# Feature-major projections as seven block products, in three passes of tokens

## The chip, the cores and the metric

The kernel runs on one core of one Trainium2 chip. TensorE (PE) multiplies: a matmul takes 128 rows of a stationary operand (loaded by LDWEIGHTS, the rows PEld of the profile) and streams up to 512 columns past it into a bank of PSUM, 128 x 512 numbers of fp32. VectorE (DVE), ScalarE (ACT) and GpSimd (POOL) work element by element, SyncE (SP) only issues DMAs. SBUF is the working memory; POOL does not touch PSUM in this kernel. Every engine has its own queue and runs it in order; semaphores join them.

The metric is device time in microseconds of one execution.

## What is computed

One layer on 2048 prompt tokens and 32 sample tokens, fp32:

```python
h = jnp.einsum('bsd,de->bse', x, w_in)              # 1024 -> 6 x 512
u, v, ga, bv, bg, gb = jnp.split(h, ...)
u = gelu(u); v = layer_norm(gelu(v), a_ln_g, a_ln_b)
y_a = u * spatial_gating(v, a_ws, a_bias) * silu(ga) # 128-token chunks, 8 heads
a = bv * sigmoid(bg)
c, new_hist = depthwise_causal_conv(conv_hist, a, b_conv_w, b_conv_b)   # 31 taps
y_b = silu(layer_norm(c, b_ln_g, b_ln_b)) * silu(gb)
y = jnp.einsum('bse,ed->bsd', concatenate([y_a, y_b]), w_out)
x_new = layer_norm(ALPHA * x + y, post_ln_g, post_ln_b)
```

Outputs are the new tokens, the last 30 convolution rows of both groups and the normalised v rows of the sample.

## The kernel before

Every fp32 operand of a product is split into a high part (an ACT copy to fp32r) and a low part (the rest, a subtraction on DVE or POOL), and a product is three matmuls: high with high, high with low, low with high.

The tokens lie in four groups of 512, 544, 512 and 512 (the sample in the second). Two halves of two groups each are worked through one after the other. In each half come the v products of the first group (token-major, `mm_v`, the tokens stationary), then bg and bv, v of the second group, and u, ga and gb. These five are feature-major (`mm_f`): 128 features of the weights are stationary, and the tokens of both groups stream past, in blocks of 512 or 272 columns, over 8 slices k of the 1024 inputs. A feature tile holds one bank per block until all 24 products of each block are done; six banks of the tag "g" are there for all products.

ACT empties u, ga, gb and bg with their functions; bv is multiplied by sigmoid(bg) on DVE into the padded rows A. `conv_pair` runs the convolution as 31 steps of 128 x 512 per feature tile (the first on ACT, 30 scalar_tensor_tensor operations on DVE), two tiles at a time, with the sums in PSUM. `ln_chain` normalises over features with column sums on PE. `spat` does the gating of v with one matmul of 256 columns for the high part of v against both parts of the weights, and one for the low part; the two halves of the 256 columns are then added by an ACT copy and a DVE addition (S<-sp,S). Results y go to DRAM (Yd). After TEND the output projection reads them back, one tile of 128 tokens at a time (`o_tile`), with the residual and the last LayerNorm on DVE.

Weights are loaded by `load_w` four steps ahead and split by `split_w`: the high part by ACT, the low part by POOL (`gtt`), the first eight on DVE (`tt`). `when(t)` gives each piece of work a due time in units of `T0`; a scheduler puts the instructions of each engine into a fixed order by these. All helpers `tt`, `gtt`, `stt` and `act` have one line each, so the profile shows their operations under L58, L64, L61 and L67. L266 and L269 are the feature products, L293 to L295 the v products, L507 and L508 the spatial gating, L659 to L661 the output projection.

## Time and profile before

| | us |
|---|---|
| three runs | 780.39, 785.9, 787.47; median 785.9 |
| profiled execution | 786.06 |
| its span, first to last instruction | 784.2 |
| mean granted TensorE clock | 0.99 |

The profile is one execution. Each row of a group gives line, engine, operation, tiles out<-in, the shape (with * between rows and columns of the stationary operand), the count, busy time, the mean duration of one in ns, and the idle time of the engine just before with what ended it. A row of the timeline gives start, length, and xN for N equal instructions in a row. Matmuls overlap, so the mean duration of one is longer than the distance between two starts.

### The profile page before, as it was taken

To read this page: it belongs to the slowest core of one execution; us is meant where nothing else is said; L and a number is where in the kernel's file an instruction comes from. 1 tells how busy PE (TensorE), PEld (TensorE's weight loads), DVE (VectorE), ACT (ScalarE), POOL (GpSimd) and SP (SyncE) were. 2 spreads that over 40 slices of the span, in tenths; PEclk is the share of its full clock that TensorE was granted. 3 is DMA by queue.
4 is the path that set the end of the run, shared out by engine and by line. 5 is a ranking of instruction groups with operands and counts; after the bars stand their busy time and mean duration, and the time that the engine had idled before them with its cause. 6 is when DMAs were issued, how large, how long until landed. Compare 5 with 4: busy or idle time off the path is not lost.

```text
span 784.2 us, 10387 instructions
## 1 busy us (share of the span) xinstructions
PE 764.3 (97%) x3799; PEld 640.6 (82%) x3799; DVE 627.7 (80%) x986; ACT 274.0 (35%) x499; POOL 260.5 (33%) x204
## 2 busy tenths in 40 slices
PE   8999999999999999999899999999989999899996
PEld 6799998799889998888688888888878888688885
DVE  5339999882799999965999996899999987955455
ACT  6562222353562234376312343551350124011100
POOL 2652122343313339451213343221213322243320
PEclk9999999999999999999999999999999999999998
DMA  9621112211125327411211311124542244354411
GB/s 296 234 67 43 41 41 52 87 53 42 37 65 172 123 81 210 114 40 43 82 53 58 95 40 54 41 94 161 176 146 70 82 150 152 141 182 161 147 54 54
DMA packets 45474, 79.12 MB, mean 101 GB/s; under 512 B 7152, under 2 KB 16496, under 8 KB 45296
## 3 DMA queue, kind: packets, MB, share of 16 engines
q1 hardware_dynamic: 45424, 78.46, 31.3%
q8 instruction: 30, 0.49, 0.3%
q14 instruction: 20, 0.16, 0.1%
HBM read 61.21 MB, written 17.23 MB: 100 GB/s over the span
## 4 chain that ended last, share of the span: by engine, by line
PE 92%; DVE 3%; ACT 2%; DMA 1%; issue 1%; POOL 0%; SPq 0%; DVEq 0%; ACTq 0%; POOLq 0%
PE f L266 37%; PE f L269 18%; PE o L659 8%; PE o L660 8%; PE o L661 8%; PE t L295 4%; PE t L294 4%; PE t L293 4%; PE sp L507 1%; DVE r L61 1%; PE sp L508 1%; DMA xr<-in_xT_dram 0%; DVE ls L406 0%; ACT A L67 0%; DVE gb L58 0%
## 5 line engine op out<-in xcount | busy, mean ns | idle before, releaser
L266 PE MATMUL f<-xs,wh 128*128 128x512 f32 (+1 forms) x1600 | 369.6, 352 | 5.3 <-DVE S L58 3.3
L61 DVE SCALAR_TENSOR_TENSOR c<-A,vec,c 128x512 f32<-128x512 f32 x464 | 319.3, 749 | 2.5 <-ACT c L67 0.6
L266 PEld LDWEIGHTS f<-xs,wh 128*128 128x128 f32 x1600 | 271.7, 189 | 48.0 <-issue 5.9
L64 POOL TENSOR_TENSOR wl<-wr,wh 128x512 fp32r<-128x512 f32 x104 | 138.6, 1335 | 320.5 <-ACT wh L145 311.1
L269 PE MATMUL f<-xs,wl 128*128 128x512 f32 (+1 forms) x800 | 214.2, 351 | 0.0
L269 PEld LDWEIGHTS f<-xs,wl 128*128 128x128 f32 x800 | 140.7, 188 | 20.4 <-issue 0.2
L145 ACT CAST wh<-wr 128x512 fp32r<-128x512 f32 x112 | 69.2, 620 | 237.1 <-PE f L266 139.5
L659 PE MATMUL o<-wo,yh 128*128 128x512 f32 (+1 forms) x264 | 103.9, 394 | 4.7 <-ACT yh L611 4.7
L660 PE MATMUL o<-wo,yh 128*128 128x512 f32 (+1 forms) x264 | 103.4, 392 | 0.0
L661 PE MATMUL o<-wo,yl 128*128 128x512 f32 (+1 forms) x264 | 97.5, 387 | 0.0
L64 POOL TENSOR_TENSOR yl<-yr,yh 128x512 fp32r<-128x512 f32 x32 | 44.9, 1411 | 83.4 <-ACT yh L611 82.2
L659 PEld LDWEIGHTS o<-wo,yh 128*128 128x128 f32 x264 | 50.6, 192 | 16.5 <-ACT yh L611 5.6
L660 PEld LDWEIGHTS o<-wo,yh 128*128 128x128 f32 x264 | 50.7, 192 | 10.7
L661 PEld LDWEIGHTS o<-wo,yl 128*128 128x128 f32 x264 | 50.0, 189 | 11.0
L611 ACT CAST yh<-yr 128x512 fp32r<-128x512 f32 x32 | 19.6, 621 | 106.9 <-PE o L660 81.4
L61 DVE SCALAR_TENSOR_TENSOR r<-r,o 128x512 f32<-128x512 f32 (+1 forms) x33 | 21.6, 666 | 42.1 <-PE o L661 42.1
L58 DVE TENSOR_TENSOR S<-sp,S 64x256 f32<-64x256 f32 (+1 forms) x68 | 27.8, 409 | 26.9 <-ACT S L513 25.2
L294 PE MATMUL t<-wl,xs 128*128 128x512 f32 x128 | 49.3, 395 | 0.0
L293 PE MATMUL t<-wh,xs 128*128 128x512 f32 x128 | 47.7, 394 | 1.4 <-ACT xs L185 1.4
L295 PE MATMUL t<-wh,xs 128*128 128x512 f32 x128 | 48.4, 397 | 0.0
L64 POOL TENSOR_TENSOR xs<-xr,xs 128x512 fp32r<-128x512 f32 (+1 forms) x24 | 31.4, 1323 | 28.3 <-ACT xs L165 28.3
L64 POOL TENSOR_TENSOR or<-or,mhalf 128x1 f32<-128x1 f32 x16 | 16.0, 1000 | 72.4 <-DVE or L639 72.2
(109 smaller groups left out, 677.7 us busy)
## 6 DMA issues: line engine op xcount, KB each, us to landing
wr<-in_wall_dram SPq DMA_DIRECT2D x112, 256.0 KB, 2.6
yr<-yd SPq DMA_DIRECT2D x64, 128.0 KB, 2.2
r<-in_xn_dram SPq DMA_DIRECT2D x16, 512.0 KB, 4.5
out_dram<-r SPq DMA_DIRECT2D x15, 512.0 KB, 2.6
xr<-in_xT_dram SPq DMA_DIRECT2D x23, 256.0 KB, 4.1
wor<-in_wall_dram SPq DMA_DIRECT2D x16, 256.0 KB, 2.8
yd<-S SPq DMA_DIRECT2D x12, 256.0 KB, 2.6
yd<-gb SPq DMA_DIRECT2D x12, 256.0 KB, 2.1
```

What stands on the lines that cost most here:

```text
L58: nc.vector.tensor_tensor(out, a, b, op=op)
L61: nc.vector.scalar_tensor_tensor(out, a, s, b, op0=op0, op1=op1)
L64: nc.gpsimd.tensor_tensor(out, a, b, op=op)
L145: nc.scalar.copy(hi, r)
L266: nc.tensor.matmul(pt[b][:, :w], hk, xsp[g, k][:, part, c0 : c0 + w], start=(k == 0 and part == 0), stop=False)
L269: nc.tensor.matmul(pt[b][:, :w], lk, xsp[g, k][:, 0, c0 : c0 + w], start=False, stop=(k == NK - 1))
L293: nc.tensor.matmul(pt[t][:m], hi[:, c0 : c0 + m], wh, start=st, stop=False)
L294: nc.tensor.matmul(pt[t][:m], hi[:, c0 : c0 + m], wl, start=False, stop=False)
L295: nc.tensor.matmul(pt[t][:m], lo[:, c0 : c0 + m], wh, start=False, stop=en)
L659: nc.tensor.matmul(p, hi, wh, start=(k == 0), stop=False)
L660: nc.tensor.matmul(p, hi, wl, start=False, stop=False)
L661: nc.tensor.matmul(p, lo, wh, start=False, stop=(k == NK - 1))
```

## The change

The five feature-major projections become block products. A unit is a pair of feature tiles of one kind (ten units: bg, bv, bg, bv, u, ga, u, ga, gb, gb). Its weights are four blocks, A11 to A22, of 128 features and 512 inputs; the tokens of a pass are four blocks, B11 to B22, of 512 inputs and half of the pass's tokens. Seven products of these blocks or of their sums (Strassen's, with the sums S1 to S4 of weights and T1 to T4 of tokens) replace eight. Each is 12 matmuls. Three passes of 768, 768 and 544 tokens replace the two halves; the sample's 32 columns lie half at the end of each half of the third pass.

```diff
+HW = [384, 384, 272]
+CONV = [72.0, 75.0, 56.0]
+PRODUCTS = [("A11", "B11", "A", True), ("A12", "B21", "B", True), ("S2", "T2", "A", False),
+            ("S3", "T3", "C", True), ("S1", "T1", "A", False), ("A22", "T4", "C", False),
+            ("S4", "B22", "A", False)]
...
-    def bank(name):
-        return ps.tile([P, W], F32, name=name, tag="g", bufs=6)
+    def bank(name, grp):
+        return ps.tile([P, W], F32, name=name, tag="g" + grp, bufs=2)
+
+    def wide(name):
+        return ps.tile([P, 2 * W], F32, name=name, tag="c", bufs=2)
...
+    def hl_tile(g):
+        wsp[g] = sx.tile([P, 2, W], F32R, name=f"w{g}", tag="w", bufs=5)
+        return wsp[g]
+
+    def split(g, raw, sub):
+        t = hl_tile(g)
+        nc.scalar.copy(t[:, 0], raw)
+        sub(t[:, 1], raw, f(t[:, 0]), SUB)
...
+        if name[0] == "A":
+            split(g, R(name), tt if (p == 0 and n < 2 and j < 2) else gtt)
+        elif p:
+            if name in ("S3", "S4"):
+                wdma[len(wdma)] = nc.sync.dma_start(f(hl_tile(g)), Sc[n, name])
+            else:
+                split(g, R(name), gtt)
+        else:
+            if name == "S2":
+                sums(p, n, "S1", R("A21"), R("A22"), tt)
+                sums(p, n, "S2", ssum[n, "S1"], R("A11"), tt)
+                sums(p, n, "S3", R("A11"), R("A21"), tt if n < 3 else gtt)
+                sums(p, n, "S4", R("A12"), ssum[n, "S2"], tt)
+            split(g, ssum[n, name], gtt)
+            if name in ("S3", "S4"):
+                nc.sync.dma_start(Sc[n, name], f(wsp[g]))
...
+        tt(t1, b12, b11, SUB)
+        tt(t2, b22, t1, SUB)
+        tt(t3, b22, b12, SUB)
+        tt(t4, b21, t2, SUB)
+        traw[p, kk] = t4
+        x_split(p, "T2", kk, t2, gtt)
+        x_split(p, "T3", kk, t3, gtt)
+        x_split(p, "T1", kk, t1, gtt)
...
+            psum[grp] = bank(f"f{grp}{p}_{n}", "A" if grp == "A" else "B")[:, : HW[p]]
+        q = psum[grp]
+        for kk in range(4):
+            x = X[p, blk, kk]
+            hk, lk = [w[:, a, kk * P : kk * P + P] for a in range(2)]
+            for m, (l, r) in enumerate(((hk, x[:, 0]), (hk, x[:, 1]), (lk, x[:, 0]))):
+                nc.tensor.matmul(q, l, r, start=(opens and kk + m == 0), stop=(kk == 3 and m == 2),
+                                 skip_group_check=not opens)
...
+        if j == 0:
+            out("open", p, i0, None)
+            take("a1", p, n, psum["A"])
+        elif j == 1:
+            tt(snap["a1"], psum["B"], snap["a1"], ADD)
+            out("11", p, i0, snap["a1"])
+        elif j == 2:
+            take("a2", p, n, psum["A"])
+        elif j == 3:
+            take("c1", p, n, psum["C"])
+        elif j == 4:
+            take("a3", p, n, psum["A"])
+            gtt(snap["a3"], snap["a3"], snap["c1"], ADD)
+            out("22", p, i0, snap["a3"])
+        elif j == 5:
+            tt(snap["a2"], psum["C"], snap["a2"], ADD)
+            out("21", p, i0, snap["a2"])
+        else:
+            out("12", p, i0, psum["A"])
+            out("close", p, i0, None)
...
+            nc.tensor.matmul(o, hi, wt[:m, h, 0], start=True, stop=False)
+            nc.tensor.matmul(o, hi, wt[:m, h, 1], start=False, stop=False)
+            nc.tensor.matmul(o, lo, wt[:m, h, 0], start=False, stop=True)
```

`take` is an ACT copy of a bank that goes on being summed into; the name a in the profile is such a copy. B and C lie in two banks of tag "gB", which the spatial gating shares; A lies in two of tag "gA"; the v products use both. In the first pass the four weight sums of a unit are made (mostly on DVE) and written to DRAM, S3 and S4 already split; the later passes read S1 and S2 raw and S3 and S4 as split pairs. A token sum T4 takes over the place of a block that has been used.

Further: convolution steps are 768 tokens wide in the first two passes and 512 in the third, over two banks (`wide`); spatial gating sums its three products in PSUM, with 128 columns each, and ACT copies the result; u * silu(ga) is formed on POOL before the product with S; bv's block 22 is multiplied on POOL; v weights are loaded anew for each half of each pass; LayerNorm of the convolution goes by halves of a pass, and for the first two passes gb waits in DRAM (gr reads it back). The output projection has its own pool of tiles, and its first four token tiles share the weights slice by slice.

On PE, a feature tile of the first half before, and the first two products of the first unit after (f and fB, fA are the banks, xs and xB the tokens, w, wh and wl the weights, sp a gating bank):

```order
L266 MATMUL f_0_441<-xs_0_80,wh_342 128x512 x2
L269 MATMUL f_0_441<-xs_0_80,wl_343 128x512
L266 MATMUL f_0_441<-xs_1_95,wh_342 128x512 x2
L269 MATMUL f_0_441<-xs_1_95,wl_343 128x512
L266 MATMUL f_0_441<-xs_2_106,wh_342 128x512 x2
L269 MATMUL f_0_441<-xs_2_106,wl_343 128x512
```

```order
L365 MATMUL fB_0_691<-xB_2_291,w_578 128x384 x3
L365 MATMUL fB_0_691<-xB_3_296,w_578 128x384 x3
L635 MATMUL sp_0_0_713<-wt,vh_0_663 128x128
L636 MATMUL sp_0_0_713<-wt,vh_0_663 128x128
L365 MATMUL fA_0_669<-xB_0_123,w_566 128x384 x3
L365 MATMUL fA_0_669<-xB_1_133,w_566 128x384 x3
```

The products are shorter and change banks after twelve, and gating matmuls stand between them with 128 columns.

On DVE, during the v products of the last group before, and at the change from the first pass to the second after (vst are statistics of v, c convolution sums, a<-fC the addition of C, t the token sums from the raw tokens x and y):

```order
L480 BN_STATS vst_0_4485<-gv_0_4477 128x6
L61 SCALAR_TENSOR_TENSOR c_3_4061<-A_3_4053,vec,c_3_4061 128x512
L480 BN_STATS vst_1_4488<-gv_1_4478 128x6
L61 SCALAR_TENSOR_TENSOR c_2_4059<-A_2_3920,vec,c_2_4059 128x512
L480 BN_STATS vst_2_4491<-gv_2_4479 128x6
```

```order
L72 TENSOR_TENSOR a_9_2296<-fC_9_2313,a_9_2296 128x384
L72 TENSOR_TENSOR t_0_2458<-x_0_1_2444,y_0_0_2454 128x384
L75 SCALAR_TENSOR_TENSOR c_3_1427<-A_3_1294,vec,c_3_1427 128x768
L75 SCALAR_TENSOR_TENSOR c_2_1425<-A_2_1292,vec,c_2_1425 128x768
L72 TENSOR_TENSOR t_0_2459<-x_4_1_2446,t_0_2458 128x384
L72 TENSOR_TENSOR t_0_2460<-x_4_1_2446,x_0_1_2444 128x384
```

Between the last addition of C of one pass and the first of the next, 16 token sums stand among 36 convolution steps and the splits of half of the v weights.

On POOL, at the same two places (wl and w are low parts of weights, vl of v, xB and xT of tokens and token sums):

```order
L64 TENSOR_TENSOR wl_4442<-wr_4421,wh_4441 128x512
L64 TENSOR_TENSOR wl_4460<-wr_4439,wh_4459 128x512
L64 TENSOR_TENSOR wl_4519<-wr_4457,wh_4518 128x512
L64 TENSOR_TENSOR wl_4551<-wr_4516,wh_4550 128x512
L64 TENSOR_TENSOR vrs_4476<-vrs_4476,mhalf 128x4
```

```order
L78 TENSOR_TENSOR xB_2_2552<-x_2_1_2548,xB_2_2552 128x384
L78 TENSOR_TENSOR w_2545<-wr_2484,w_2545 128x512
L78 TENSOR_TENSOR xB_2_2555<-x_6_1_2550,xB_2_2555 128x384
L78 TENSOR_TENSOR xT_1_2525<-t_1_2518,xT_1_2525 128x384
L78 TENSOR_TENSOR xT_1_2528<-t_1_2519,xT_1_2528 128x384
L78 TENSOR_TENSOR w_2604<-wr_2543,w_2604 128x512
```

Splits of tokens and token sums now stand between those of the weights.

More of the change, by code (lines that the diff above doesn't have):

```diff
@@ new lines, in hymba_step_kernel, with store_y, place, ev_plain @@
+    Yd = {(p, k): dr.tile([P, TMAX], F32, name=f"yd{p}_{k}") for p in range(3) for k in range(8)}
+    def store_y(p, k, src):
+        nc.sync.dma_start(Yd[p, k][:, : 2 * HW[p]], src)
+    At, E = {}, {}
+    later = [[], [], []]
+    def place(which, p, i0):
+        c0 = HW[p] * (which[1] == "2")
+        return i0 + (which[0] == "2"), slice(c0, c0 + HW[p])
+    def ev_plain(kind, func):
+        def out(which, p, i0, q):
+            if which == "open":
+                for i in (i0, i0 + 1):
+                    E[kind, i] = work(f"{kind}{p}_{i}")
+            elif which == "close":
+                for i in (i0, i0 + 1):
+                    DONE[kind](p, i)
+            else:
+                i, s = place(which, p, i0)
+                act(E[kind, i][:, s], q, func)
+        return out
@@ new lines, in temp, with colsum, ln_chain @@
+    def temp(p, name, dtype=F32):
+        if p < 2:
+            return sx.tile([P, W], dtype, name=name, tag="sw", bufs=4)[:, : HW[p]]
+        return sb.tile([P, TMAX], dtype, name=name, tag="t", bufs=8)[:, : HW[p]]
+    def colsum(nm, hl):
+        q = wide(nm)[:, : hl[0].shape[1]]
+        nc.tensor.matmul(q, ones, hl[0], start=True, stop=False)
+        nc.tensor.matmul(q, ones, hl[1], start=False, stop=True)
+        return q
+    def ln_chain(p, t):
+        if p == 2:
+            conv_sample(p)
+        for h in range(2):
+            ln_half(p, h, t + 6 * h)
+        later[p] = None
@@ new lines, in hymba_step_kernel, with done_ga, ev_v @@
+    S = {}
+    chunks, vsp = {}, {}
+    def done_ga(p, i):
+        w = 2 * HW[p]
+        u, e = E["u", i][:, :w], E["ga", i][:, :w]
+        gtt(u, u, e, MUL)
+        s = S[p][:, i, :w]
+        tt(s, s, u, MUL)
+        store_y(p, i, s)
+    def ev_v(p, half, pt):
+        n = len(pt)
+        nt = PW[p] // P
+        five = n > nt
+        t0 = T0[cur["h"] + 1]
+        mv = sb.tile([P, 4, 2], F32, name=f"vmv{p}_{half}", tag="mv", bufs=2)
+        rs = sb.tile([P, 2, 4], F32, name=f"vrs{p}_{half}", tag="rs", bufs=2)
+        if five:
+            nc.gpsimd.memset(mv, 1.0)
+        gv = [work(f"gv{p}_{half}_{t}")[:, :W] for t in range(n)]
+        rows = [P] * nt + [NS] * five
+        when(t0 - 0.5)
+        for t, m in enumerate(rows):
+            e = gv[t][:m]
@@ L574, in ev_gb @@
[L574 to L589 removed]
+                act(e, pt[t], AF.Gelu)
@@ new lines, in hymba_step_kernel @@
+    for p in range(3):
+        plan_pass(p)
+    for j in range(4, 8):
+        at(1.5 * (j - 3), lambda j=j: x_plain(0, j, 0, tt))
+    at(12, setup)
+    loaded = prepped = 4
+    for h in range(NSTEP):
+        cur["h"], cur["t"] = h, T0[h]
+        while loaded < min(NSTEP, h + LOAD_AHEAD + 1):
+            when(T0[h] - PRE)
+            load_w(loaded)
+            loaded += 1
+        while prepped < min(NSTEP, h + SPLIT_AHEAD + 1):
+            when(T0[h] - PRE)
+            prep_w(prepped)
+            prepped += 1
+        run_todo(h)
+        when(T0[h])
+        if steps[h][0] == "v":
+            mm_v(h)
+        else:
+            mm_f(h)
+            when(T0[h + 1] - 0.5)
+            after_f(h)
@@ L592, in hymba_step_kernel @@
+    cur["h"], cur["t"] = NSTEP, TEND
+    run_todo(NSTEP)
+    assert not todo, todo
+    stage.close()
+    so = ctx.enter_context(tc.tile_pool(name="so", bufs=1, side="right", reuse_waits="tile"))
+    pgb = so.tile([P, 2, D], F32, name="pgb")
     wo, yh, R = {}, {}, {}
```

896 lines of the change are left out of this document (422 added, 474 removed).

## The prediction

> **What bounds the kernel now.** First the page's busy times and its chain of work that ended last.
>
> ```profile
> span 784.2 us, 10387 instructions
> PE 764.3 (97%) x3799; PEld 640.6 (82%) x3799; DVE 627.7 (80%) x986; ACT 274.0 (35%) x499; POOL 260.5 (33%) x204
> PE 92%; DVE 3%; ACT 2%; DMA 1%; issue 1%; POOL 0%; SPq 0%; DVEq 0%; ACTq 0%; POOLq 0%
> ```
>
> The matmul stream is the bound: 97% busy and 92% of the chain. Second the windows of the three stages (first group and half of the projections, second half, output projection), to see who stands close behind it.
>
> ```profile
> 36.00:348.00 312.00, 311.79 (x1820) 274.63 (x1818) 255.20 (x409) 126.38 (x246) 121.48 (x93) 1.00 0.27 80
> 348.00:584.00 236.00, 231.12 (x1016) 188.65 (x1016) 212.98 (x324) 95.41 (x170) 63.11 (x48) 0.99 0.27 84
> 584.00:784.00 200.00, 189.41 (x828) 152.90 (x828) 143.08 (x222) 32.47 (x52) 61.34 (x49) 0.97 0.36 121
> ```
>
> The columns after the length are PE, PEld, DVE, ACT and POOL busy, the granted clock, and the DMA share with GB/s. In the two projection stages DVE is busy 468 of 548 us (85%), POOL 185 of 548 (34%). So DVE is a near second; POOL is far from full. That PE hardly waits there has a reason in the code: only the bv columns and one half of each spatial-gating bank need DVE to be freed, the other eviction is ACT's.
>
> **What the blocks save on PE.** A matmul's mean duration includes its drain, so I take start-to-start times from the timeline: 512-wide feature matmuls, and the 256-wide ones of the last output tile (first and last of 48).
>
> ```profile
> 411.10 0.62 PE L269 MATMUL f<-xs,wl 128*128 128x512 f32 x2
> 411.56 1.09 PE L266 MATMUL f<-xs,wh 128*128 128x512 f32 x4
> 412.49 0.39 PE L269 MATMUL f<-xs,wl 128*128 128x512 f32 x1
> ...
> 771.22 0.28 PE L659 MATMUL o<-wo,yh 128*128 128x256 f32 x1
> ...
> 776.76 0.28 PE L661 MATMUL o<-wo,yl 128*128 128x256 f32 x1
> ```
>
> Six 512-wide ones take 412.49 - 411.10 = 1.39 us, 0.232 each; 47 steps of 256 take 5.54 us, 0.118 each. The line through both is 0.0045 us + 0.444 ns a column: 0.125 us at 272, 0.175 at 384, 0.061 at 128. Now the counts.
>
> ```profile
> L266 PE MATMUL f<-xs,wh 128*128 128x512 f32 x960 | 299.8, 395 | 5.3 <-DVE S L58 3.3 <-DVE Bc L61 1.4 <-DVE A L58 0.6
> L269 PE MATMUL f<-xs,wl 128*128 128x512 f32 x480 | 166.3, 394 | 0.0
> L266 PE MATMUL f<-xs,wh 128*128 128x272 f32 x640 | 127.5, 288 | 0.0
> L269 PE MATMUL f<-xs,wl 128*128 128x272 f32 x320 | 67.4, 287 | 0.0
> L507 PE MATMUL sp<-wt,vh 128*128 128x256 f32 x64 | 14.6, 283 | 0.1
> L508 PE MATMUL sp<-wt,vl 128*128 128x256 f32 x64 | 14.0, 281 | 0.0
> ```
>
> Feature products before: 1440 x 0.232 + 960 x 0.125 = 454 us. After: 30 units of 7 products of 12 matmuls, 1680 of them 384 wide and 840 272 wide: 294 + 105 = 399. The saving is 55 us. The v products and the output projection keep their matmuls. Spatial gating goes from 144 matmuls of 256 (17 us) to 216 of 128. No row shows one that narrow. By the line it is 0.061 each, 13 us in all; if a weight load could not be hidden it would be the 0.19 us that one LDWEIGHTS lasts, 41 us. I take the line, since 256-wide ones already run at 0.118 under loads of 0.19, and keep 28 us for the other end. On PE alone the kernel would so lose 55 + 4 = 59 us.
>
> **What the blocks cost the other engines.** The seven products don't give finished outputs: per unit a DVE addition with B, one with C and a POOL addition (60 + 30), ACT copies of A1, A2, A3 and C1, ten times four weight sums (33 on DVE), and per pass sixteen token sums on DVE with their splits on POOL. DVE loses the 68 additions S of spatial gating and one gate product. Prices come from runs of equal instructions.
>
> ```profile
> 311.55 6.67 DVE L61 SCALAR_TENSOR_TENSOR c<-A,vec,c 128x512 f32<-128x512 f32 x10
> 344.93 2.87 DVE L58 TENSOR_TENSOR A<-A,mu 128x272 f32<-128x272 f32 x8 [2.60 <-PE mu L379]
> 367.58 2.62 DVE L58 TENSOR_TENSOR A<-A,ls 128x544 f32<-128x544 f32 x4
> ...
> L61 DVE SCALAR_TENSOR_TENSOR r<-r,or,pgb 128x1024 f32<-128x1024 f32 x15 | 19.1, 1281 | 0.7
> ...
> L64 POOL TENSOR_TENSOR xs<-xr,xs 128x512 fp32r<-128x512 f32 x16 | 20.6, 1306 | 7.3 <-ACT xs L165 7.3
> L64 POOL TENSOR_TENSOR xs<-xr,xs 128x544 fp32r<-128x544 f32 x8 | 10.8, 1356 | 21.0 <-ACT xs L165 21.0
> ```
>
> A convolution step of 512 costs 0.66 to 0.69 us (I use 0.69, with the switches between operations); with the row at 1024 a step of 768 is 0.96. Two-operand DVE additions are 0.35 at 272, 0.47 at 384, 0.60 at 512. POOL is 1.31 at 512 and, on the slope of its two rows, 1.10 at 384 and 0.93 at 272. With these prices the rows of the changed program sum to 633 us on DVE and 484 us on POOL (before: 600 and 252 in the same way). The convolution alone hardly changes, 240 x 0.96 + 120 x 0.69 = 313 against 480 x 0.69 = 331.
>
> **How DVE and POOL disturb each other.** This is what decides, and the trace shows it at one place.
>
> ```profile
> 166.78 3.15 POOL L64 TENSOR_TENSOR vl<-gv,vh 128x512 fp32r<-128x512 f32 x2 [4.58 <-ACT vh L493]
> 169.90 3.45 POOL L64 TENSOR_TENSOR wl<-wr,wh 128x512 fp32r<-128x512 f32 x2
> ...
> 167.10 1.68 DVE L58 TENSOR_TENSOR ls<-ls,ls 128x512 f32<-128x512 f32 x1
> 168.71 1.78 DVE L58 TENSOR_TENSOR S<-S,u 128x512 f32<-128x512 f32 x1
> 170.41 1.79 DVE L58 TENSOR_TENSOR lr<-ls,lr 128x512 fp32r<-128x512 f32 x1
> ...
> L58 DVE TENSOR_TENSOR S<-S,u 128x512 f32<-128x512 f32 x12 | 14.1, 1192 | 15.6 <-ACT u L67 15.6
> L58 DVE TENSOR_TENSOR ls<-ls,ls 128x512 f32<-128x512 f32 x12 | 12.1, 1008 | 0.1
> L58 DVE TENSOR_TENSOR lr<-ls,lr 128x512 fp32r<-128x512 f32 x6 | 5.6, 927 | 2.8 <-ACT lr L417 2.8
> L58 DVE TENSOR_TENSOR gb<-gb,A 128x512 f32<-128x512 f32 x12 | 9.5, 805 | 1.9 <-ACT gb L67 1.9
> L58 DVE TENSOR_TENSOR A<-A,ls 128x512 f32<-128x512 f32 x12 | 8.0, 727 | 0.0
> L58 DVE TENSOR_TENSOR A<-f,sg 128x512 f32<-128x512 f32 x12 | 8.0, 687 | 5.7 <-PE f L269 5.6
> ```
>
> With both operands in SBUF a DVE operation of 0.69 us lasts 1.7 to 1.8 while POOL runs, and POOL's own pairs stretch from 2.6 to 3.15 and 3.45 us: they take turns. With one operand in PSUM (A<-f,sg, and the convolution) nothing is added. Over the 54 quoted instructions of the first kind the excess over 0.687 is 12 x 0.505 + 12 x 0.321 + 6 x 0.24 + 12 x 0.118 + 12 x 0.04 = 13.2 us, 0.25 each, with POOL a third busy. In the changed program POOL has 417 us of its 484 before the output stage, about 70% of it. Twice the share gives 0.5; I take 0.45, with 0.2 (nothing grows) and 0.65 (half a POOL operation, at every one) as ends. Until the output there are 233 such additions on DVE, 180 of them after the first unit.
>
> The Trainium skill (SBUF — State Buffer, Who interferes with whom) says that a DVE instruction with two SBUF inputs contends with GpSimd reads and that the later one blocks for the whole instruction. By that rule a burst of additions that meets a full POOL queue would pay nearly 1.3 us each, and the 180 would cost 234 us instead of my 81. The trace agrees on the turns, and its 0.25 shows that most arrive at a free port.
>
> **The sum.** The order of the changed program places every addition that empties a B or C bank, so DVE and POOL work can be summed between the additions of C that end each unit. A bank pool of two lets PE run ahead of them by about half a unit, no more. Each stretch takes the longest of its engines: PE; DVE with 0.45 per addition of two SBUF operands; POOL with those additions' own length.
>
> ```profile
> 4.15 0.71 PE L293 MATMUL t<-wh,xs 128*128 128x512 f32 x1
> 13.71 1.36 POOL L64 TENSOR_TENSOR xs<-xr,xs 128x544 fp32r<-128x544 f32 x1 [13.20 <-ACT xs L165]
> ```
>
> Up to the end of the first unit: PE 4.15 until its first weight matmul, and 52; POOL's 43.5 us start near 13, where its first split stood before, and meet some additions: I take 62.
> Units 2 to 10: PE 134, DVE 118 + 18 = 136, POOL 117 + 24 = 141: 138, as POOL may be late by its reserve of five weight buffers.
> To the end of unit 11, with the v products of pass two: PE 51, DVE 52.5 + 11 = 63, POOL 52 + 12 = 64: 63.
> Units 12 to 20: PE 135, DVE 119 + 21 = 140, POOL 107: 140.
> To the end of unit 21: PE 40, DVE 45 + 9 = 54, POOL 53: 54.
> Units 22 to 30: PE 97.5, DVE 106 + 22 = 128, POOL 97: 128.
> Together 585. Taken unit by unit with the same prices it is 619, since a unit with two gate products or a LayerNorm is long on DVE or POOL and its neighbour on PE; buffers level most of that, and I add 10. After unit 30 PE has 188 us (the output projection); DVE has 154 + 18 there, so it is hidden.
>
> ```profile
> L659 PE MATMUL o<-wo,yh 128*128 128x512 f32 x248 | 99.4, 402 | 4.7 <-ACT yh L611 4.7
> ...
> 779.66 1.53 DVE L61 SCALAR_TENSOR_TENSOR r<-r,or,pgb 128x512 f32<-128x512 f32 x3
> ```
>
> Keep the waits of that stage, 5 us, and the 7 us from the end of the last matmul (777.0) to the span's 784.2, as the last tile is written as before: 595 + 188 + 5 + 7 = 795, and 797 with the 1.9 us that the profiled execution (786.06) has around its span. It stands on the runs' median of 785.9.
> ```profile
> L145 ACT CAST wh<-wr 128x512 fp32r<-128x512 f32 x112 | 69.2, 620 | 237.1 <-PE f L266 139.5 <-issue 52.9 <-PE t L295 22.2
> ```
>
> ACT (an estimate of 460 us, with 0.62 us at 512 and less where narrower) stays at or below PE in every stretch; I cost it at nothing, and if it loses that cover its copies of A hold a bank each. The weights now move some 146 MB, 183 GB/s on average against 101 now; slices of 296 GB/s exist.
>
> ```profile
> GB/s 296 234 67 43 41 41 52 87 53 42 37 65 172 123 81 210 114 40 43 82 53 58 95 40 54 41 94 161 176 146 70 82 150 152 141 182 161 147 54 54
> ```
>
> So transfers hide if they are asked for in time; SP issues them in one line, and a store that waits for late DVE work holds the weight loads behind it.
>
> **The rivals.** One: PE stays the bound. If two-operand additions wait 0.2 us as now and nothing is uneven, the stretches are 58, 134, 58, 135, 50 and 117, together 552, and the time 754; PE alone would be 58 + 134 + 51 + 135 + 40 + 97.5 = 516, hence 718. For it speaks that PE waited only 5 us for DVE in all feature products; against it that DVE's own rows already exceed PE's in units 22 to 30. It decides from a wait below about 0.3 each. Two: the delays add up, at 0.65 a wait and unit by unit; the stretches are 66, 146, 70, 150, 58, 138, with 10 more 638, and the time 840; SP's line of stores and the narrow matmuls (28 us at most on PE, hardly half of it exposed) push the same way. Against it: a late DVE leaves POOL idle, which frees the port. Three: every addition waits for a whole POOL operation, as the three in the timeline nearly did; 180 x (1.31 - 0.45) = 155 us more, some 950. The 0.25 of the groups speaks against it. It is what the Trainium skill's rule on the ports (SBUF — State Buffer, Who interferes with whom) would give for a queue that is always full.
>
> **How the numbers follow.** The forecast, 780 to 830, gets 0.50; rival one (718 to 778) 0.34; rival two (830 to 870) 0.13; rival three 0.03. The lines for 1% are 778 and 794, about what a measurement can tell from no change. Faster is rival one and a little of the forecast's lower edge, 0.36; within 1% is 0.19 of the forecast; the rest of it with rivals two and three is 0.45. The range 748 to 840 leaves about one in ten on each side; 780 to 830 is the forecast's own.
>
> **What would show it.** Right: PE busy falls below 92% of the span, with its waits put down to DVE additions of B and C and to POOL splits, most at the two starts of a pass and in pass three; the S and t additions last over 0.9 us on average. Wrong: feature matmuls not at 0.175 us, additions near 0.5 us, or PE waits on DMA or ACT instead. The narrow matmuls' spacing tells 0.061 from 0.19.

## The result and the profile after

The changed kernel takes 825.95 us (median of four runs, 823.94 to 827.9) against 786.17 for the one before on the same chip: 1.052 times as long, 95% interval 1.046 to 1.058. The forecast was 797, 11 us more than before; 40 us more were measured. Direction and range hold; the size is short by 29 us.

From the page of the changed kernel: span, busy times, and the chain by engine.

```profile
span 826.2 us, 12087 instructions
PE 746.0 (90%) x3995; PEld 672.5 (81%) x3995; DVE 722.4 (87%) x999; ACT 429.2 (52%) x822; POOL 509.6 (62%) x403
PE 29%; DVE 8%; DMA 3%; ACT 2%; issue 1%; POOL 1%; SPq 0%; DVEq 0%; POOLq 0%; ACTq 0%
```

PE's busy share fell from 97% of the span to 90%. The last row has to be read with care: its shares are of the span and add up to 44%, because the chain could be followed back only to 451 us. Of the stretch that it covers PE has two thirds, where it had 92% of the whole before. Now the seven stretches of the forecast (to the end of unit 1, 10, 11, 20, 21, 30, and of the span), with the columns of the windows shown before.

```profile
0.00:76.70 76.70, 62.51 (x262) 50.53 (x263) 58.85 (x84) 49.58 (x93) 46.44 (x41) 0.89 0.65 210
76.70:217.30 140.60, 136.68 (x797) 134.76 (x796) 129.51 (x141) 82.14 (x156) 123.44 (x90) 1.00 0.53 179
217.30:287.10 69.80, 57.96 (x265) 48.35 (x264) 69.70 (x86) 41.94 (x78) 58.51 (x48) 0.95 0.60 180
287.10:432.10 145.00, 140.87 (x802) 138.81 (x801) 123.24 (x157) 92.46 (x173) 87.37 (x66) 0.98 0.60 187
432.10:486.60 54.50, 46.03 (x232) 35.89 (x232) 54.50 (x73) 34.64 (x82) 44.45 (x44) 0.97 0.55 172
486.60:619.70 133.10, 112.60 (x802) 109.71 (x801) 116.34 (x188) 81.81 (x163) 76.90 (x62) 0.87 0.58 184
619.70:826.20 206.50, 189.38 (x847) 154.48 (x845) 170.28 (x275) 46.67 (x80) 72.49 (x58) 0.97 0.45 152
```

| stretch, ends with | unit 1 | 10 | 11 | 20 | 21 | 30 | span |
|---|---|---|---|---|---|---|---|
| forecast, us | 62 | 138 | 63 | 140 | 54 | 128 | 200 |
| measured, us | 77 | 141 | 70 | 145 | 54.5 | 133 | 206.5 |

The misses add to 41 us. The forecast's 10 us for unevenness and the 2 us by which the profiled execution lies above the median leave 29. In the third and fifth stretch DVE is busy throughout. In the sixth, and in the first, nobody is.

PE's own time is as costed where the rows bore on it, and not at the narrow matmuls. Three places of PE's timeline: full-rate units, narrow matmuls at full clock and, in pass three, at half clock.

```profile
127.73 1.72 PE L365 MATMUL fC<-xT,w 128*128 128x384 f32 x9
129.29 0.51 PE L365 MATMUL fB<-xB,w 128*128 128x384 f32 x2
...
80.04 0.28 PE L636 MATMUL sp<-wt,vh 128*128 128x128 f32 x1
80.15 0.28 PE L637 MATMUL sp<-wt,vl 128*128 128x128 f32 x1
80.26 0.27 PE L635 MATMUL sp<-wt,vh 128*128 128x128 f32 x1
...
493.78 0.33 PE L635 MATMUL sp<-wt,vh 128*128 128x128 f32 x1 [1.56 <-ACT vh L621]
...
496.97 0.82 PE L365 MATMUL fA<-xB,w 128*128 128x272 f32 x2 [2.52 <-ACT bg L81]
...
498.12 0.41 PE L637 MATMUL sp<-wt,vl 128*128 128x128 f32 x1
498.33 0.41 PE L635 MATMUL sp<-wt,vh 128*128 128x128 f32 x1
```

Nine products of 384 take 129.29 - 127.73 = 1.56 us, 0.173 each (0.175 forecast). The 128-wide ones start 0.11 us apart, 0.21 at half clock; the forecast had 0.061. 216 x 0.05 is 11 us. Summing all spacings in this way, PE's own work fell by 48 us, not 59. Against that stand 21 us more of matmuls slowed by a half clock (25 against 5) and 67 us more of waits (84 against 18); this accounting closes to within 3 us of the 42 us between the spans.

What PE waits for, in all, the first rows:

```profile
PE fA L365 <- ACT a L351: 14.4, 5, 9.8
PE fB L365 <- DVE w L72: 6.9, 1, 6.9
PE v L336 <- ACT xB L226: 4.5, 2, 2.5
PE v L336 <- ACT gv L81: 4.4, 2, 2.3
PE fC L365 <- DMA w<-cS: 4.3, 3, 1.7
PE o L789 <- DVE wo L72: 3.2, 1, 3.2
```

The additions that empty the B and C banks, which the forecast feared, come to 2.9 us further down the list. Its head is split weights and tokens that are late (w, xB, cS), and one wait of 9.8 us. Summed over the whole list by the engine that ended them, the waits are ACT's for 40 of 72 us, DVE's for 20, POOL's for 8 and late transfers' for 4 (PE's idle time alone; the 84 above hold shorter delays too). The second row is this piece of DVE's timeline in the first unit:

```profile
46.50 1.50 DVE L72 TENSOR_TENSOR w<-wr_A,w 128x512 fp32r<-128x512 f32 x1
47.92 1.50 DVE L72 TENSOR_TENSOR sS<-wr_A,wr_A 128x512 f32<-128x512 f32 x1
49.35 1.37 DVE L72 TENSOR_TENSOR t<-y,t 128x384 f32<-128x384 f32 x1
50.64 1.49 DVE L72 TENSOR_TENSOR sS<-sS,wr_A 128x512 f32<-128x512 f32 x1
52.05 1.47 DVE L72 TENSOR_TENSOR sS<-wr_A,wr_A 128x512 f32<-128x512 f32 x1
53.45 1.34 DVE L72 TENSOR_TENSOR t<-x,x 128x384 f32<-128x384 f32 x1
54.72 1.75 DVE L72 TENSOR_TENSOR sS<-wr_A,sS 128x512 f32<-128x512 f32 x1
56.39 1.75 DVE L72 TENSOR_TENSOR w<-wr_A,w 128x512 fp32r<-128x512 f32 x1
```

Eight operations that last 0.54 to 0.68 us undisturbed last 1.34 to 1.75. POOL is busy without a break here, and every one waits for most of a POOL operation: 0.8 us beside those of 384 columns (1.0 undisturbed), 1.1 beside those of 512 (1.3). The last is the low part of A12, for which PE stands 6.9 us. The 9.8 us wait is in pass three:

```profile
546.78 0.44 PE L492 MATMUL var<-lr,ones 128*128 128x384 f32 x1
548.75 2.57 DVE L530 RECIPROCAL ls<-ls 128x192 f32<-128x192 f32 x2 [0.35 <-ACT ls L81]
551.81 1.95 DVE L72 TENSOR_TENSOR A<-A,ls 128x384 f32<-128x384 f32 x4
554.97 1.44 POOL L78 TENSOR_TENSOR A<-a,bg 128x256 f32<-128x256 f32 x1 [12.16 <-DVE gr L72]
556.44 0.22 ACT L429 COPY hist<-A 128x30 f32<-128x30 f32 x1 [0.83 <-POOL A L78]
556.56 0.38 ACT L351 COPY a<-fA 128x272 f32<-128x272 f32 x1
556.99 1.73 PE L365 MATMUL fA<-xB,w 128*128 128x272 f32 x6 [9.77 <-ACT a L351]
557.07 0.55 DVE L72 TENSOR_TENSOR gr<-gr,A 128x384 f32<-128x384 f32 x1
```

The second half of pass two's LayerNorm still holds A buffers that pass three's bv products need. Behind it stand a POOL product into A, a copy of the convolution's history (hist) on ACT that waits for this product, ACT's copy of a bank, and PE.

### The profile page after: what moved, and what is told of

Its sections match the earlier page's. It is cut to its first block, busy times and chain, and to the rows that moved or that the text cites. A ratio compares the mean times of both kernels' runs of the same rounds, so it can differ in the third digit from the quotient of the medians.

```text
span 826.2 us, 12087 instructions
## 1 busy us (share of the span) xinstructions
PE 746.0 (90%) x3995; PEld 672.5 (81%) x3995; DVE 722.4 (87%) x999; ACT 429.2 (52%) x822; POOL 509.6 (62%) x403
## 5 line engine op out<-in xcount | busy, mean ns | idle before, releaser
L75 DVE SCALAR_TENSOR_TENSOR c<-A,vec,c 128x768 f32<-128x768 f32 (+1 forms) x348 | 304.2, 920 | 2.2 <-ACT c L81 1.5
L78 POOL TENSOR_TENSOR w<-wr_A,w 128x512 fp32r<-128x512 f32 x86 | 124.1, 1449 | 55.7 <-ACT w L175 40.8
L365 PE MATMUL fA<-xB,w 128*128 128x384 f32 (+1 forms) x720 | 132.4, 328 | 16.7 <-ACT a L351 9.8
L365 PEld LDWEIGHTS fA<-xB,w 128*128 128x128 f32 x720 | 119.1, 195 | 19.8 <-ACT a L351 10.0
L365 PE MATMUL fA<-xT,w 128*128 128x384 f32 (+1 forms) x720 | 128.4, 328 | 4.7 <-ACT a L351 4.6
L365 PE MATMUL fC<-xT,w 128*128 128x384 f32 (+1 forms) x720 | 126.7, 324 | 5.0 <-DMA w<-cS 4.3
L365 PEld LDWEIGHTS fA<-xT,w 128*128 128x128 f32 x720 | 118.9, 195 | 6.2 <-ACT a L351 5.8
L365 PEld LDWEIGHTS fC<-xT,w 128*128 128x128 f32 x720 | 117.1, 192 | 6.1 <-DVE gr L72 2.0
L789 PE MATMUL o<-wo,yh 128*128 128x512 f32 (+1 forms) x264 | 102.7, 389 | 5.6 <-DVE wo L72 3.2
L788 PE MATMUL o<-wo,yh 128*128 128x512 f32 (+1 forms) x264 | 100.3, 389 | 4.4 <-ACT wo L731 2.9
L790 PE MATMUL o<-wo,yh 128*128 128x512 f32 (+1 forms) x264 | 101.7, 387 | 0.0
L365 PE MATMUL fB<-xB,w 128*128 128x384 f32 (+1 forms) x360 | 72.0, 335 | 10.7 <-DVE w L72 6.9
L175 ACT CAST w<-wr_A 128x512 fp32r<-128x512 f32 x90 | 55.5, 616 | 49.9 <-PE fA L365 18.2
L789 PEld LDWEIGHTS o<-wo,yh 128*128 128x128 f32 x264 | 50.4, 191 | 16.6 <-DVE wo L72 3.7
L78 POOL TENSOR_TENSOR or<-or,mhalf 128x1 f32<-128x1 f32 x16 | 14.9, 930 | 72.8 <-DVE or L777 72.8
```

What stands on the lines that cost most here:

```text
L75: nc.vector.scalar_tensor_tensor(out, a, s, b, op0=op0, op1=op1)
L78: nc.gpsimd.tensor_tensor(out, a, b, op=op)
L175: nc.scalar.copy(t[:, 0], raw)
L365: nc.tensor.matmul(q, l, r, start=(opens and kk + m == 0), stop=(kk == 3 and m == 2), skip_group_check=not opens)
L788: nc.tensor.matmul(p, hi, wh, start=(k == 0), stop=False)
L789: nc.tensor.matmul(p, hi, wl, start=False, stop=False)
```

## Experiments: whose time it is

Theory one is the forecast's: DVE's own work and its waits for POOL bound PE. The rivals are ACT's order, buffers, late transfers. Times below without an interval are one execution. First DVE is relieved of half the convolution, and then POOL's reads are taken away.

```diff
 # half_taps
-        for j in range(1, TAPS):
+        for j in range(2, TAPS, 2):
 # fill_for_split: in split and x_split, where sub is gtt
-        sub(t[:, 1], raw, f(t[:, 0]), SUB)
+        nc.gpsimd.memset(f(t[:, 1]), 0.0)
 # fill_long: two whole fills and one of 3/8 of the width
```

> Every second convolution step is left out (180 of 360, 120 at 0.92 us and 60 at 0.66: 150 us of DVE); the output is not the reference's. Theory one (DVE's queue, with its turns against POOL, is what PE waits for): the stretches in which DVE is full shrink towards PE's own time. End of unit 10 to 11 from 69.9 to 58 us, end of 20 to 21 from 54.5 to 46, units 22 to 30 from 133 to 112; units 2 to 10 and 12 to 20 stay within 4 us of 140 and 145, the first unit at 77; together 775 to 785 us. Rival (ACT's order, the five A buffers and late weight loads hold PE): all stretches stay within 3 us of the changed kernel's, 815 to 826 us.

> POOL's subtractions that make the low part of split weights and tokens become fills with zero, so the low parts are zero and the output is not the reference's; DVE, ACT, PE and the transfers keep every instruction. POOL reads almost nothing from SBUF before the output stage. If the turns at SBUF are a large part of the loss: DVE additions with two SBUF operands fall from some 0.9 to 0.65 us on average, the stretch to the end of unit 11 from 70 to 60 us, that to unit 21 from 54.5 to 48, units 22 to 30 from 133 to 118, units 2 to 10 from 140.5 to 136: 785 to 800 us. If DVE's own work is the bound and the turns are small: additions faster, but less than 10 us gained, 816 to 826. If ACT or late transfers bound: nothing gained, 820 to 828.

> As in the run with fills, but each of POOL's subtractions becomes three fills (whole, whole and three eighths of the width), so that POOL is as long in it as in the subtraction (by the 0.53 us of a fill at 512 some 1.3 us, by the 0.42 at 384 some 1.1); the low parts are zero and the output is not the reference's. POOL's time in its queue is back, its turns with DVE at SBUF are not. If the 30 us that the single fills gained came from the turns: the time stays at 794 to 804 us, the stretch to the end of unit 11 at 55 to 60. If they came from the length of POOL's queue: 815 to 826 us, that stretch at 66 to 72. Between the two, the share of each is read from that stretch.

Half the taps: 820.33 us, and not the 775 to 785 of theory one. The stretch to unit 11 is 72.8 us and that to unit 21 is 56.8, no shorter; units 22 to 30 fall from 133 to 112. Fills: 796.12 us; long fills: 804.44. Their stretches to unit 11 are 55.5 and 56.3 us; their units 22 to 30 stay at 132 and 135 (118 were expected of the fills). Windows of the third and sixth stretch with half the taps, then of the third with long fills:

```profile
222.10:294.90 72.80, 57.24 (x267) 47.39 (x266) 55.35 (x71) 52.18 (x94) 55.19 (x44) 0.93 0.55 176
...
501.20:613.40 112.20, 101.79 (x794) 99.58 (x793) 69.47 (x115) 66.64 (x141) 76.18 (x63) 0.97 0.62 200
```

```profile
208.60:264.90 56.30, 54.46 (x273) 48.24 (x272) 53.99 (x77) 41.21 (x78) 43.10 (x110) 0.97 0.62 198
```

So a full DVE was no proof that DVE's own work is the bound: the stretch lasts 73 us with DVE busy for 55, and 56 us with DVE busy for 54 when POOL does not read. Part of the reason is that the freed time drew pass one's LayerNorm into the stretch (its reciprocals move from 312 to 250 us), whose operations take turns with POOL, which convolution steps do not (one of 768 columns lasts 1.01 us on average in the changed kernel and 1.02 beside the long fills). The group rows of the token sums, changed kernel and long fills, show the turns alone:

```profile
L72 DVE TENSOR_TENSOR t<-y,t 128x384 f32<-128x384 f32 x8 | 9.6, 1195 | 0.0
L72 DVE TENSOR_TENSOR t<-x,x 128x384 f32<-128x384 f32 x8 | 9.5, 1188 | 0.0
```

```profile
L72 DVE TENSOR_TENSOR t<-y,t 128x384 f32<-128x384 f32 x8 | 4.4, 550 | 0.1
L72 DVE TENSOR_TENSOR t<-x,x 128x384 f32<-128x384 f32 x8 | 4.4, 550 | 0.0
```

The span falls by 23.5 us, from 826.2 to 802.7, with POOL nearly as long in its queue as before (457 against 510 us). The three starts gain 9.4, 13.6 and 5.8 us (the stretches to units 1, 11 and 21), and 5 us are lost again in between. Not all of it is shown to be the turns'. A fill does not read, but it does not wait for ACT's cast either: in the changed kernel POOL's splits of weights stand 78 us in all behind that cast, and the fills in their place do not, and the raw tiles come free sooner. What the additions themselves lose, over the shortest of their kind, falls from 16.6, 10.7 and 9.1 us in the three stretches to 1.8, 1.1 and 0.5. In the second and third DVE was full, so there the turns account for most of the gain. The length of POOL's work is worth the next 8 us, by one execution of each kernel.

## Experiments: spatial gating, and the gap in pass three

```diff
 # sp256: for two heads at a time, in a bank of its own
-            nc.tensor.matmul(o, hi, wt[:m, h, 0], start=True, stop=False)
-            nc.tensor.matmul(o, hi, wt[:m, h, 1], start=False, stop=False)
-            nc.tensor.matmul(o, lo, wt[:m, h, 0], start=False, stop=True)
+            nc.tensor.matmul(o, hi, wt[:m, h], start=True, stop=False)
+            nc.tensor.matmul(o, lo, wt[:m, h], start=False, stop=True)
...
+                tt(o, q4[r, :, 1, :P], o, ADD)
 # hist_close: the copy under "close" in place of "open"
+                nc.scalar.copy(At[p, i][:, :HIST], hist[:, i, :])
 # abuf6
-... tag="A", bufs=5)
+... tag="A", bufs=6)
```

> Spatial gating alone goes back to the form of the kernel before: 144 matmuls of 256 columns in place of 216 of 128, two banks per pair of chunks, each emptied by a copy on ACT and an addition on DVE. If DVE bounds PE wherever it is near full: PE's own time falls by 7 us (216 x 0.112 to 144 x 0.118), DVE gains 68 additions of 0.35 to 0.4 us, 25 us, in the units behind the start of each pass: 826 to 840 us. If the narrow matmuls are what the forecast lost on PE and DVE has room there: 812 to 820 us.

> The copies of the convolution's history into A move from the opening of a bv unit to its close; nothing else changes. In pass three PE stands 10.2 us in the unit bv 2 (from 546.8 us on) behind an ACT copy a that stands in ACT's queue behind such a history copy, which waits for a free A buffer. If ACT's order makes that wait: the gap falls below 4 us, the half clock after it goes too, 812 to 817 us. If the missing A buffer itself makes it: the gap stays within 2 us, now put to the DVE product into A, and the time stays at 822 to 828 us.

> Six A buffers in place of five (and four buffers in place of five for raw tokens and for copies of banks, to make room). If the missing buffer makes the 10.2 us gap in unit bv 2 of pass three: bv 0 opens without waiting and the gap shrinks or moves back by what one buffer is worth, 810 to 820 us. If the late convolution and LayerNorm of pass two make it, so that even six are not free in time: the gap stays, 822 to 830 us; and if the two tags that gave room now hold, above 830.

sp256: 841.48 us, 1.068 times the kernel before (1.065 to 1.071), 15 us worse than the change as it is. PE waits for the new additions (first row of its waits):

```profile
PE sp L639 <- DVE S L72: 21.1, 13, 4.4
```

That part of the change is therefore a gain, though the narrow matmuls cost twice what was forecast. hist_close: 825.82, ratio 1.049 (1.046 to 1.052); the gap stays at 10.2 us (from the start of the last matmul before it to the next). This does not clear ACT's order. The edit changed it in pass one alone; from 130 us on ACT's instructions stand in the order that they had. At the gap the bank copy still follows the history copy that waits for POOL:

```profile
554.33 0.22 ACT L429 COPY hist<-A 128x30 f32<-128x30 f32 x1 [0.83 <-POOL A L78]
554.45 0.38 ACT L351 COPY a<-fA 128x272 f32<-128x272 f32 x1
```

In the changed kernel PE's last matmuls into A banks before the gap were done by 539 us, and the copy started at 556.56, when ACT came to it. Whether the gap closes when the copy stands earlier in ACT's queue was not tried. abuf6: 829.29, ratio 1.056 (1.051 to 1.060); the gap halves to 4.7 us, while the tags that gave room now hold elsewhere (in the first unit ACT waits 8.5 us for raw tokens, 2.4 before). That one decides nothing about the total.

```diff
 # conv_early
-CONV = [72.0, 75.0, 56.0]
+CONV = [72.0, 68.0, 56.0]
 # plain3: in pass three
+PLAIN = [("A11", "B11", "A", True), ("A12", "B21", "A", False), ...]   # eight products
 # ln_tail_out
-        var = colsum(f"var{p}_{h}", (hi, lo))
+        if (p, h) != (1, 1): ...   # column sum, root, reciprocal
```

> The convolution of pass two is planned over 68 us a pair in place of 75, so that its end and the LayerNorm behind it are asked for 14 us earlier; nothing else changes. If the 10.2 us gap in unit bv 2 of pass three, and the half clock behind it, come from the A buffers that this LayerNorm and its gates free late: units 22 to 30 go from 133 to 118 to 123 us, units 12 to 20 stay within 3 us of 145, together 810 to 818 us. If the gap has another cause, or the earlier convolution only delays the additions that empty banks: 822 to 832 us.

> Pass three goes back to eight products of the four blocks, without sums of tokens and weights; passes one and two stay as they are. PE has 120 more matmuls of 272 columns, 15 us; POOL loses 16 token splits, 10 weight splits and 10 additions, DVE 16 token sums and 20 additions of banks. If what stops PE in pass three comes from the seven-product form: end of unit 20 to 21 from 54.5 to 46 us, units 22 to 30 from 133 to 118, together 800 to 806 us. If it comes from what pass two leaves behind (late LayerNorm, A buffers): that gap of 10 us stays and the 15 us of PE come on top, 822 to 838 us.

> In the second half of pass two's LayerNorm alone the variance's column sum, its root and its reciprocal are left out (the columns are scaled by the sum of squares itself), so that part of the output is not the reference's; its two matmuls on PE fall away with it. If PE's 10.2 us gap is the tail of this LayerNorm, from the variance to the last gate: some 6 us of the tail go (root 1.4 with a table load, reciprocals 2.6, casts and waits), the gap falls to 3 to 5 us, the half clock behind it shrinks, units 22 to 30 go from 133 to 122 to 127 us, together 815 to 821 us. If the gap has another cause: it stays above 8 us and the time at 823 to 828 us.

conv_early: 829.19, ratio 1.054 (1.051 to 1.057). It tested nothing: on every engine the order of the instructions came out the same from end to end, and so did the gap. The 3 us between it and the changed kernel are what two measurements of one order can differ by. plain3: 825.91, ratio 1.052 (1.049 to 1.056), as the second case expects: 15 us more PE, less work elsewhere, and a wait of 9.5 us still there, ended by a product on DVE:

```profile
541.98 3.31 PE L383 MATMUL fA<-xB,w 128*128 128x272 f32 x13 [9.48 <-DVE Asm L78]
```

Pass three of this kernel makes no such copies of banks, so one is not needed for the gap. The gap is pass two's, not the seven products' of pass three. In eleven kernels (the changed one among them) a gap of 10.2 us stands there, and PE resumes 0.6 to 1.2 us before the end of pass two's last gate (gr), wherever that gate falls between 524 and 567 us. In the kernels where pass two's convolution ended before unit 21 did (half_taps, sp256 and the later presplit_sv, half_taps_t and half_taps_fill) it is not there. ln_tail_out: 821.62, ratio 1.042 (1.037 to 1.047); the wait falls to 5.2 us and units 22 to 30 to 128.7, a little short of the 122 to 127 expected. A weight load just before it comes 1.9 us later than in the changed kernel (3.45 against 1.58 us of wait):

```profile
543.73 3.09 PE L365 MATMUL fC<-xT,w 128*128 128x272 f32 x12 [3.45 <-DMA w<-cS]
552.01 3.09 PE L365 MATMUL fA<-xB,w 128*128 128x272 f32 x12 [5.20 <-ACT a L351]
```

## Experiments: relieving POOL, DVE, or both

```diff
 # presplit_sv: S1, S2 and the split v weights kept in DRAM and loaded
+            wdma[len(wdma)] = nc.sync.dma_start(f(hl_tile(g)), Sc[n, name])
+                wdma[len(wdma)] = nc.sync.dma_start(f(hl_tile(g)), Vc[j])
 # t_on_dve; combo is this with S1, S2 kept split; combo2 is combo and conv_early
-        x_split(p, "T2", kk, t2, gtt)    # T3, T1 likewise
+        x_split(p, "T2", kk, t2, tt)
 # half_taps_t: half_taps and t_on_dve; half_taps_fill: half_taps and fill_for_split
 # token_sums_out
+        t1, t2, t3 = b12, b22, b11
 # weight_sums_out
+                for s in ("S2", "S3", "S4"):
+                    ssum[n, s] = ssum[n, "S1"]
```

> The split v weights and the split sums S1 and S2 are kept in DRAM as S3 and S4 are, and loaded instead of being split again. Per pass two and three 40 POOL splits of weights fewer in units, 8 fewer on POOL and 8 on DVE among the v products, 8 fewer on DVE in pass one; casts of ACT with them. All output is computed. Theory now (at the start of a pass POOL's splits, with their turns against DVE, pace everything, DVE waiting for POOL's buffers): end of unit 10 to 11 from 70 to 60 us or less, 20 to 21 from 54.5 to 48, first unit 77 to 73, together 800 to 810 us. Theory one (DVE's own work): 820 or more. Rival, transfers: PE waits for loads of w, 4 us now, grow above 10 us and take back what is gained, 815 to 835.

> The low parts of the token sums T1, T2, T3 (12 splits a pass) move from POOL, 1.1 us each at 384 columns, to DVE, 0.47 us. Theory now: two-SBUF operations of DVE and POOL pass one gate in turns, so their undisturbed durations add; in the changed kernel that sum is 70 us in the first stretch of 77, 139 of 140, 66 of 70 in the stretch with the v products of pass two and 52 of 54.5 in that of pass three. Moving the twelve makes it 7.6, 7.6 and 6.6 us shorter: first unit 77 to 70, end of unit 10 to 11 from 70 to 64, end of 20 to 21 from 54.5 to 49, together 808 to 815 us. Theory one (DVE's own queue, full there) expects DVE 5.6 us longer in each: 75 and 59 us, together 830 to 842.

> S1 and S2 are kept split in DRAM as S3 and S4 are (40 POOL splits and casts fewer, 15 MB more moved), and the low parts of T1 to T3 are made on DVE. All output is computed. By the sum at the gate: first unit 77 to 70 us, unit 11 from 70 to 62, unit 21 from 54.5 to 49, units 12 to 20 from 145 to 140, units 22 to 30 from 133 to 114 (as in the run with split sums and split v weights), units 2 to 10 at 140, the end as before: 780 to 795 us. If DVE's queue bounds the starts of a pass, or loads of w come late: 810 or more.

> Every second convolution step is left out, as in the run with half the taps, and the low parts of T1 to T3 are made on DVE, as in the run with those alone; the output is not the reference's. Alone, the one left the stretch to the end of unit 11 at 72.8 us, the other at 69.0. If DVE's queue and the shared gate stand at equal height there, both together lower both: 60 to 64 us, unit 21 from 54.5 to 49, total 790 to 805. If something else holds PE there: 68 to 72 and 54 to 57 us, total 815 to 822.

> Half the convolution steps left out and POOL's low parts of weights and tokens filled with zero: neither DVE nor the gate nor the late LayerNorm should hold PE. If these three are the whole of what PE waits for before the output stage: stretches of 66, 136, 54, 138, 43, 102 us and 206 for the output, together 745 to 760 us, half clock below 6 us. If ACT's order, late transfers or the two banks of a group hold it too: 775 or more.

> Three of the four sums of token blocks are left out (T1 to T3 are split from the raw blocks themselves); 12 DVE additions of two SBUF operands fewer per pass, the output is not the reference's. That lowers DVE's queue by 12 x 0.47 us and their turns, and the gate by 5.6 us, at the start of each pass. Equal height: first unit 77 to 70, unit 11 from 70 to 62, unit 21 from 54.5 to 49, together 803 to 812 us (the gap in pass three stays). If POOL's queue alone or ACT's order holds the start of a pass: within 3 us in each stretch, 818 to 828.

> Of the four sums of weight blocks only S1 is made, and split four times; 30 additions fewer in pass one (23 on DVE, 7 on POOL), the output is not the reference's. If these sums, standing in DVE's queue ahead of the low part of A12 and stretched by their turns, make the 6.9 us wait for it: the wait falls below 3 us, first unit 77 to 70; units 2 to 10 from 140.5 to 137, as PE alone needs 136; together 812 to 819 us. If that wait has another cause: first unit 75 or more, 820 to 827.

| us | total | to unit 1 | 11 | 20 | 21 | 30 |
|---|---|---|---|---|---|---|
| changed kernel | 825.95 | 77 | 70 | 145 | 54.5 | 133 |
| presplit_sv | 815.3 | 84 | 68 | 140 | 58.5 | 114 |
| t_on_dve | 840.66 | 74 | 69 | 155 | 56 | 135 |
| combo | 836.66 | 74 | 70 | 143 | 59 | 136.5 |
| half_taps_t | 812.01 | 71.5 | 72 | 147 | 57 | 111.5 |
| half_taps_fill | 771.37 | 74 | 56 | 142 | 51 | 103 |
| token_sums_out | 812.79 | 69 | 65 | 143.5 | 49 | 134 |
| weight_sums_out | 817.68 | 72 | 68 | 141 | 55.5 | 132 |

presplit_sv (ratio 1.039, 1.035 to 1.044) is the fastest version with all output, and still slower than before and than the 800 to 810 expected. It gains where pass two's convolution ends earlier (471 us against 505), and loses in the first unit, where PE waits 10.3 us for the column sums of the spatial weights. None of the three starts came down to the 73, 60 and 48 us expected. In the stretch to unit 11 the additions lose 3.4 us in place of 10.7, and yet it is only 2 us shorter: PE now waits there 3.5 us for loads of split v weights (6.6 in all) and 4.5 for ACT to empty the banks of v. So fewer turns alone do not make a start short. t_on_dve (1.068, 1.065 to 1.072) refutes the theory that only the sum of both engines' reading time at a shared gate counts: that sum fell by 7.6 us (as worked out ahead) and the stretch to unit 11 by 1, since DVE is full there, as this row of its third stretch shows:

```profile
214.90:283.90 69.00, 56.46 (x264) 47.03 (x263) 69.00 (x90) 41.16 (x76) 42.49 (x35) 0.98 0.53 169
```

combo (1.065, 1.061 to 1.068) falls on the second side of what was expected: DVE is full at the starts, and its convolution in pass two ends at 503 us, so the gap stays at 10.2. combo2, with that convolution planned earlier, is within 2 us of it (834.71, ratio 1.061, 1.057 to 1.065); like conv_early it tested nothing, since the order of every engine came out the same. half_taps_t was to decide whether DVE and the gate stand at equal height; by its own terms the answer is no, for the stretch to unit 11 stays at 72, with DVE 69% and POOL 65% busy. PE stands 6.3 us there for one low part on POOL, and POOL itself was idle for the cast on ACT:

```profile
251.24 1.30 POOL L78 TENSOR_TENSOR w<-wr,w 128x512 fp32r<-128x512 f32 x1 [6.20 <-ACT w L175]
```

So besides the two queues there is a chain of sums, casts and low parts through three in-order queues; this is read from the trace and was not tried by itself, and no run takes work from ACT alone. The starts became shorter where additions were left out: token_sums_out has 12 fewer a pass and gains 7, 5 and 6 us at the three starts (7, 8 and 5.5 were expected). That takes DVE's work, its turns and a link of the chain away at once and does not tell them apart. weight_sums_out gains 4 at the first, where the wait for A12 falls from 6.9 to 2.1 us, and nothing in units 2 to 10, which are within 5 us of PE's own 136.

half_taps_fill shows what remains when turns, POOL's length, its waits for casts and late LayerNorm are all gone: 771 us, 16 less than the kernel before (787.1 in the run beside it), not the 745 to 760 expected. ACT ends 26 of the 36 us that PE still waits. The first unit is still 74 us long, with a granted clock of 0.91:

```profile
0.00:74.00 74.00, 64.45 (x274) 52.45 (x275) 44.57 (x86) 50.94 (x96) 22.70 (x43) 0.91 0.69 225
```

## Why the prediction was off

The rise was forecast as 11 us and measured as 40. The steps that failed are the sum of the first unit (15 us short), the 10 us for all that is late or uneven, which buffers were to level, and the half clock and ACT, both put at nothing.

- **PE's saving.** Feature products as forecast: 0.173 us at 384, 0.125 at 272. The term for spatial gating was mis-sized: the line through 256 and 512 columns gave 0.061 at 128, the spacing is 0.112, within the bounds named (0.19). 11 us. The Trainium skill (TensorE: Matmul & The Clock Gate, LDWEIGHTS) takes the time of a weight load by its columns alone, 128 / 1.2 = 107 ns for 128; the spacing is close to that. The Trainium skill's sustained 81 ns for 128 columns (TensorE: Matmul & The Clock Gate, Back-to-back issue gap) is not what this trace shows.
- **Turns at SBUF.** The mechanism holds: with POOL's reads of weights and tokens gone, its waits for their casts gone too, and its queue nearly as long, the span fell by 23.5 us. The size of a turn was put too high. Until the output, additions behind unit 1 lose 0.3 us each on average and not 0.45 (over the shortest of their kind), and 0.4 at the later two starts. Rival three's picture, each addition waiting for a whole POOL operation, is nearly true for bursts there and not on average. The Trainium skill's rule (SBUF — State Buffer, Who interferes with whom), the later one blocks for the whole instruction, fits the eight rows from 46.50 us on. POOL's own prices, taken on a slope from 512 and 544 columns, were too high: the shortest of the changed kernel are 0.99 us at 384 and 0.76 at 272, against 1.10 and 0.93.
- **The first unit**, 62 against 77, is the worst step. The working took POOL's path as the bound: it let POOL's 43.5 us start near 13 and "meet some additions". POOL did start at 12.8 us and was busy for 46. But it is 53 additions before the first unit ends, and the last of them stand in DVE's queue ahead of the weights that PE needs next: that is the wait of 6.9 us at 58 us. The long fills, without POOL's reads and its waits for casts, gained 9 of the 15 us; the rest may lie with ACT's late tokens and a clock of 0.89, which no run tried.
- **Units 2 to 10, unit 11, 12 to 20, unit 21** came out 2.5, 7, 5 and 0.5 us above the sums. Taking the longest of DVE and POOL, both with the waits in, was nearly right there. Why was in part wrong: the trace names additions of B and C for only 2.9 us of waits, and mostly weights, tokens and copies that come late. To units 11 and 21 DVE's queue was full, waits included; where it was not, in half_taps_t, the chain through ACT held PE for as long.
- **Units 22 to 30**, 128 against 133, and "unevenness" at 10. Here DVE's queue was no bound: additions lost 9 us, not 22, and DVE is 87% busy. The step that failed is the one that took a buffer pool to level what is late. Five A buffers join two passes, and the LayerNorm of one stops the next: 133 becomes 111 to 114 in half_taps, half_taps_t and presplit_sv, where pass two's convolution ended before unit 21 did.
- **The half clock** was not costed at all, since the profile before shows 0.99. 21 us more. Every piece of it begins near waits, as in the two windows around the rows quoted at 546.78 and 493.78 us:

```profile
546.00:560.00 14.00, 3.89 (x15) 3.38 (x16) 13.32 (x24) 8.74 (x17) 3.67 (x3) 0.62 0.46 150
...
491.00:509.00 18.00, 13.91 (x79) 13.18 (x78) 15.64 (x27) 10.40 (x22) 7.28 (x5) 0.61 0.27 80
```

  No run was made that changes the clock alone, so its 21 us are a reading of the trace, and how much of them lay on the path stays open.
- **ACT** was costed at nothing because its busy time stays below PE's, as it does (429 us in all). But busy time is not lateness: 40 of PE's 72 us of waits end with an instruction on ACT, 9.8 of them behind the LayerNorm and the rest in pieces of 3 us or less. How much of that is ACT's own order, and how much it passes on from DVE, POOL and transfers, stays open.
- **The output**, 200 against 206.5: 6.5 us more than before, with waits of 2.4 to 3.2 us for its first weights on ACT, DVE and POOL and half clock behind them. No run touched this.
- **Signs named ahead.** PE below 92%: right. Sums of weights and tokens above 0.9 us: right on average (groups from 0.58 to 1.34). Waits put to additions of B and C: wrong, and to POOL's splits: 8 us. PE waiting for ACT was named as a sign against, and it appears, as said above.

## What to carry to other kernels

A saving of matmuls is worth its time only as long as PE stays the bound: here 48 us went, and three things that were hidden under PE came out, worth 20 us or so each and in part the same ones: work bunched at the starts, a LayerNorm that holds the next pass, and a clock that falls behind waits. Two engines that add up sums from SBUF share more than their busy times say, so count their two-operand instructions together at the place where they bunch, and test a full engine by taking its neighbour's reads away before taking its work, with the neighbour's waits left as they were. Before a test of an order is read, look in its trace whether the order changed at the place that matters: in hist_close, conv_early and combo2 it had not. Where one pass hands buffers to the next, follow the last reader of the buffer, not the average load.
